# Ten feed-forward blocks by seven products, and the residual added inside PSUM

## The chip, the cores and the metric

The kernel runs on one core of a Trainium2 chip. The metric is the device time of one execution in microseconds. Five engines work side by side, each through its own queue in order: TensorE (PE in the profile; its weight loads are shown apart as PEld), VectorE (DVE), ScalarE (ACT), GpSimd (POOL), and SyncE (SP), which here only issues transfers. Matmuls write to PSUM, an accumulator memory of eight banks, each holding a 128x512 fp32 tile; VectorE and ScalarE read and write it as they do the main on-chip memory, SBUF.

## The reference

Two layers of a hybrid decoder trunk on 256 tokens with a model width of 2048, all in fp32. Cut to what matters here:

```python
for l in range(DEPTH):                       # 2
    h = rms_norm(x, norm1_g[l])
    z = h @ w_in[l]
    ...                                      # gating unit and windowed attention
    x = x + mixed @ w_out[l]
    h2 = rms_norm(x, norm2_g[l])
    x = x + (jax.nn.silu(h2 @ w_gate[l]) * (h2 @ w_up[l])) @ w_down[l]
```

The feed-forward width is 5632, that is, 11 blocks of 512 columns. The change is all in the last line: how `h2 @ w_gate` and `h2 @ w_up` are multiplied out, and how the product with `w_down` is added to x.

## The kernel before

**Precision.** A matmul takes its operands as rounded fp32 (`F32R`). To keep fp32 accuracy every operand is split into a rounded part and the remainder, and a product is three matmuls: high by high, high by low, low by high (`mm3`, lines 133 to 136). Weights are split on the chip: `split2` (line 89) has ScalarE write the rounded part `wh` (line 95) and VectorE the remainder `wl` (line 96), for a loaded piece `raw` of 128 x 1024. There are six `raw`, five `wh` and four `wl` buffers.

**The unit.** `unit` (line 138) loads one piece, splits it and multiplies it with two activation blocks for both halves of the tokens: 12 matmuls of 128x512. `product` (line 152) strings units to an accumulation over the whole depth.

**Stages of a layer.** The w_in products with attention and gating between them; the w_out products (`add_part`, line 527), each added to the residual `xres` by VectorE; then the feed-forward part. `norm_block` (line 478) sums the squares of a finished piece of x on ScalarE and transposes it for the next product.

**Seven products.** The gate and up products of one block, with tokens in two halves, make a 2 x 2 product of blocks. `seven` (line 564) computes it with seven block products in place of eight, after a scheme of Strassen's kind: five products need sums of weights (VectorE, lines 590, 591 and 596; a sixth operand is completed by an accumulating transfer that POOL issues, line 598) and sums of activations (`ext`, made once in `combine`). They go in half-units of 6 matmuls (`s_unit`): four steps of five half-units into five PSUM banks `m0` to `m4`, then eight half-units into two further tiles `n0` and `n1`. At the end ScalarE and VectorE combine the banks (lines 607 to 615, 628 to 631), apply Silu, and the two results `sg` are transposed and split again by `act_T` (line 550), into one of eight `aT` buffers.

**Standard work.** Blocks 0 and 1 are done with eight products by `gate_up` (line 651). `down` (line 666) multiplies finished blocks with w_down: for each of four column groups n it takes a pair of accumulators, runs two units per block, and VectorE adds the pair onto `xres` (line 685). While the seven-product stream runs, these accumulators come from the pool `pd`, which holds one pair (`dacc`); after it they come from `pa` (`acc`).

**What sets the order.** The seven-product stream loads VectorE more than TensorE; standard units load TensorE more. The two are interleaved by a running debt: `vec` adds the estimated VectorE time of an instruction to it (1.14 or 0.6 us), `pe` takes off the matmul time (0.227 us each times `LOAD`, 0.95). Whenever the debt is over zero after a half-unit, units of the standard stream are written in. The standard stream runs in a fixed sequence, `STD_ORDER` (line 43): gate-up of block 0, down of 0 and 2, gate-up of 1, then four more downs. A down whose blocks aren't ready gives nothing. `later` and `tick` write delayed work (the transposes) in after a count of units. On top of this order the framework's scheduler places each engine's instructions.

Of the kernel before, what the change touches and what calls it, by code (L numbers as in the profile page):

```python
# [12 lines left out]
F32 = mybir.dt.float32  # L13
# [3 lines left out]
ALU = mybir.AluOpType  # L17
# [33 lines left out]
UNIT_AT = (6, 9, 12, 15, 19, 23)  # L51

# [12 lines left out]
def trunk(ctx, tc, x, xt, w_in, w_out, w_gate, w_up, w_down, sgu_w, sgu_g, consts,  # L65
# [39 lines left out]
    def vec(n, cost=VEC):  # L105
        debt[0] += n * cost
# [7 lines left out]
    def later(delay, fn):  # L114
        pending.append((clock[0] + delay, next(serial), fn))
# [8 lines left out]
    def new_acc(pool=pa, tag="acc"):  # L124
        return [pool.tile([P, NB], F32, tag=tag, name=f"{tag}{t}") for t in range(NTOK)]
# [7 lines left out]
    def mm3(acc, ah, al, wh, wl, first, last):  # L133
        nc.tensor.matmul(acc, ah, wh, start=first, stop=False)  # L134
        nc.tensor.matmul(acc, ah, wl, start=False, stop=False)  # L135
        nc.tensor.matmul(acc, al, wh, start=False, stop=last)  # L136

    def unit(src, acts, acc, first, last):
        raw = raw_load(src, 2 if clock[0] < 4 else 1)
        wh, wl = split2(raw)  # L140
        for j in range(2):
            act, aj = acts[j]
            for t in range(NTOK):
                ts = slice(t * P, (t + 1) * P)
                mm3(
                    acc[t], act[:, 0, aj, ts], act[:, 1, aj, ts], wh[:, j, :], wl[:, j, :],
                    first and j == 0, last and j == 1,
                )
        pe(12)
        tick()  # L150
# [100 lines left out]
    for lay in range(L):  # L251
# [305 lines left out]
            pe(2)  # L557
            pairs_f.setdefault(b, []).append(pair)

        def act_later(b, sg, act_T=act_T):  # L560
            for c in range(2):
                later(2 + c, lambda c=c: act_T(b, c, sg))

        def seven(b, lay=lay, pairs2=pairs2, ext2=ext2, act_later=act_later):
            bank = [pa.tile([P, NB], F32, tag="acc", name=f"m{i}") for i in range(5)]

            def s_unit(raw, m, i, op, first, last):
                wh, wl = split2(raw)
                for j in range(2):
                    ah, al = (op(2 * i + j, h) for h in range(2))  # L570
                    mm3(bank[m], ah, al, wh[:, j, :], wl[:, j, :], first and j == 0, last and j == 1)
# [34 lines left out]
            m1 = zp.tile([P, NB], F32, tag="z", name="m1")  # L606
            nc.scalar.copy(m1, bank[0])
            u1 = zp.tile([P, NB], F32, tag="z", name="u1")
            nc.vector.tensor_tensor(u1, bank[3], m1, ALU.add)
            c22 = zp.tile([P, NB], F32, tag="z", name="c22")  # L610
            c21 = zp.tile([P, NB], F32, tag="z", name="c21")
            nc.vector.tensor_tensor(c21, bank[2], u1, ALU.add)
            nc.vector.tensor_tensor(c22, bank[1], c21, ALU.add)
            nc.vector.tensor_tensor(u1, bank[1], u1, ALU.add)
            nc.vector.tensor_tensor(u1, bank[4], u1, ALU.add)
            vec(5, VEC_P)
            yield
            bank = [pa.tile([P, NB], F32, tag="acc", name=f"n{i}") for i in range(2)]
            for i in range(4):
                b21 = raw_load(w_gate[lay, b, i, 1])  # L620
                first, last = i == 0, i == 3
                s_unit(b21, 0, i, a_op(1, 0), first, last)
                yield
                s_unit(kept[i], 1, i, a_op(1, 1), first, last)
                yield
            sg = [m1, c21]
            for t, m in ((0, m1), (1, c21)):
                nc.vector.tensor_tensor(m, bank[t], m, ALU.add)
                nc.scalar.activation(m, m, AF.Silu, scale=rstd2[t])
            for t, c in ((0, u1), (1, c22)):  # L630
                nc.vector.scalar_tensor_tensor(sg[t], c, nrstd2[t], sg[t], ALU.mult, ALU.mult)
            vec(4, VEC_P)
            act_later(b, sg)
            yield

# [27 lines left out]
            vec(NTOK, VEC_P)  # L663
            act_later(b, sg)

        def down(blocks, final, lay=lay, pairs_f=pairs_f, norm_block=norm_block, ss1=ss1, pairs1=pairs1):
            for n in range(ND):
                while any(len(pairs_f.get(b, [])) < 2 for b in blocks):
                    yield False
                acc = new_acc() if seven_done[0] else new_acc(pd, "dacc")  # L670
                for k, b in enumerate(blocks):
                    for c in range(2):
                        pair = pairs_f[b][c]
                        unit(
                            w_down[lay, b, n, c], [(pair, 0), (pair, 1)], acc,
                            k == 0 and c == 0, k == len(blocks) - 1 and c == 1,
                        )
                        yield True
                for t in range(NTOK):
                    parts = 2 if final and lay == L - 1 and n == ND - 1 else 1  # L680
                    w = NB // parts
                    for i in range(parts):
                        cs = slice(n * NB + i * w, n * NB + (i + 1) * w)
                        xs = xres[:, t, cs]
                        nc.vector.tensor_tensor(xs, acc[t][:, i * w : (i + 1) * w], xs, ALU.add)  # L685
                        if final and lay == L - 1:
                            nc.sync.dma_start(out[t * P : (t + 1) * P, cs], xs)
                    vec(1, VEC_P)
                if final and lay < L - 1:
                    norm_block(n, ss1, pairs1, lay + 1, C_G1)  # L690

        def std_stream(gate_up=gate_up, down=down):
# [105 lines left out]
```

## Time and profile before

| | us |
|---|---|
| median of 3 runs | 1981.08 |
| lowest and highest | 1977.15, 1983.19 |
| the profiled execution | 1970.47 |
| its span, first to last instruction | 1968.8 |

The profile is of one execution. Its page begins with each engine's busy time in the span, and the clock that TensorE was granted in 40 slices (9 is 90% or more). A group row gives line, engine, operation, output and inputs, count, then the total busy time and the mean duration in ns of one, then the idle time of the engine just before and what ended it. Window rows give, for a stretch, the busy time and count of each engine in the order PE, PEld, DVE, ACT, POOL, then the clock, the DMA engines' busy share and their GB/s. Timeline rows give start and length in us, and in brackets an idle time before with what ended it. Durations of neighbours on one engine can overlap, so what an instruction costs its queue is the distance between two starts.

### The profile page before, as it was taken

The numbers are of one execution on the slowest core, as the hardware profiler recorded it, in microseconds if no ns is written. First come the engines' busy times: TensorE is split into PE (matmuls) and PEld (weight loads), VectorE is DVE, ScalarE is ACT, GpSimd is POOL, SyncE is SP. The second block draws the span as 40 slices with busy tenths as digits, with TensorE's granted clock in tenths as the row PEclk, the third lists the DMA queues.
The fourth block names the chain that finished last, engine by engine and source line by source line (L and its number), as shares of the span: only waits on it lengthen the run. The fifth ranks groups of instructions, "written<-read, shape, count | busy, mean of one in ns | idle before, by whom it ended". The sixth has DMA issues, their size and how long they took to land.

```text
span 1968.8 us, 24956 instructions
## 1 busy us (share of the span) xinstructions
PE 1942.7 (99%) x8884; PEld 1586.9 (81%) x8884; DVE 1678.4 (85%) x1812; ACT 1175.8 (60%) x1489; POOL 115.5 (6%) x116
## 2 busy tenths in 40 slices
PE   9999999999999999999999999999999999999999
PEld 6788888778887878888887888878788878888887
DVE  6665689999999999999856666899999999999996
ACT  7565566555565565565656755665656555655563
POOL 0210000000000000000002000000000000000000
PEclk9999999999999999999999999999999999999999
DMA  9544557667767668668555355576686776686684
GB/s 354 188 144 153 189 171 243 206 204 245 231 220 244 221 212 258 220 223 259 202 202 195 127 170 178 178 253 193 214 258 213 225 254 206 210 279 203 221 270 141
DMA packets 117805, 422.20 MB, mean 214 GB/s; under 512 B 13104, under 2 KB 13744, under 8 KB 117680
## 3 DMA queue, kind: packets, MB, share of 16 engines
q1 hardware_dynamic: 105264, 375.52, 53.2%
q0 software_dynamic: 12416, 45.09, 12.3%
q8 instruction: 69, 1.13, 0.2%
q14 instruction: 56, 0.46, 0.1%
HBM read 418.47 MB, written 2.10 MB: 214 GB/s over the span
## 4 chain that ended last, share of the span: by engine, by line
PE 85%; DVE 6%; issue 3%; ACT 2%; DMA 2%; POOL 1%; SPq 0%; DVEq 0%; ACTq 0%; POOLq 0%
PE dacc L134 9%; PE dacc L135 9%; PE dacc L136 9%; PE acc L135 8%; PE acc L136 8%; PE acc L134 8%; PE m L135 7%; PE m L136 7%; PE m L134 7%; PE n L135 3%; PE n L136 3%; PE n L134 3%; DVE wl L96 3%; ACT wh L95 1%; DVE raw L596 1%
## 5 line engine op out<-in xcount | busy, mean ns | idle before, releaser
L95 ACT CAST wh<-raw 128x1024 fp32r<-128x1024 f32 (+1 forms) x778 | 799.9, 1049 | 627.4 <-DVE raw L590 227.3
L96 DVE TENSOR_TENSOR wl<-raw,wh 128x1024 fp32r<-128x1024 f32 (+1 forms) x778 | 927.0, 1217 | 154.5 <-PE acc L135 75.9
L134 PE MATMUL dacc<-wh,aT 128*128 128x512 f32 x608 | 237.0, 392 | 0.2
L135 PE MATMUL dacc<-wl,aT 128*128 128x512 f32 x608 | 237.0, 390 | 0.0
L136 PE MATMUL dacc<-wh,aT 128*128 128x512 f32 x608 | 236.7, 390 | 0.0
L135 PE MATMUL m<-wl,ext 128*128 128x512 f32 x576 | 227.5, 395 | 4.7 <-DVE wl L96 4.7
L134 PE MATMUL m<-wh,ext 128*128 128x512 f32 x576 | 226.8, 394 | 4.8 <-ACT wh L95 4.8
L136 PE MATMUL m<-wh,ext 128*128 128x512 f32 x576 | 224.5, 390 | 0.0
L96 DVE TENSOR_TENSOR wl<-t,wh 128x1024 fp32r<-128x1024 f32 x144 | 175.5, 1219 | 16.0 <-issue 7.0
L95 ACT CAST wh<-t 128x1024 fp32r<-128x1024 f32 x144 | 151.4, 1051 | 49.5 <-PE dacc L136 31.6
L134 PE MATMUL acc<-wh,hT 128*128 128x512 f32 x448 | 179.4, 403 | 0.8 <-ACT wh L95 0.6
L135 PE MATMUL acc<-wl,hT 128*128 128x512 f32 x448 | 176.4, 394 | 1.2 <-DVE wl L96 1.1
L136 PE MATMUL acc<-wh,hT 128*128 128x512 f32 x448 | 175.6, 392 | 0.0
L598 POOL DMA_DIRECT2D t<-in_w_gate_dram x72 | 61.6, 855 | 1373.3 <-DVE wl L96 719.4
L134 PE MATMUL acc<-wh,aT 128*128 128x512 f32 x352 | 139.1, 395 | 0.0
L136 PE MATMUL acc<-wh,aT 128*128 128x512 f32 x352 | 137.3, 390 | 0.0
L135 PE MATMUL acc<-wl,aT 128*128 128x512 f32 x352 | 137.3, 390 | 0.0
L134 PEld LDWEIGHTS dacc<-wh,aT 128*128 128x128 f32 x608 | 114.1, 188 | 25.6 <-DVE xres L685 2.3
L135 PEld LDWEIGHTS m<-wl,ext 128*128 128x128 f32 x576 | 108.1, 188 | 32.0 <-DVE wl L96 10.7
L135 PEld LDWEIGHTS dacc<-wl,aT 128*128 128x128 f32 x608 | 114.2, 188 | 24.1 <-DVE wl L96 0.8
L136 PEld LDWEIGHTS dacc<-wh,aT 128*128 128x128 f32 x608 | 114.2, 188 | 23.7
L134 PEld LDWEIGHTS m<-wh,ext 128*128 128x128 f32 x576 | 108.2, 188 | 29.8 <-ACT wh L95 7.7
(145 smaller groups left out, 2974.3 us busy)
## 6 DMA issues: line engine op xcount, KB each, us to landing
raw<-in_w_gate_dram SPq DMA_DIRECT2D x176, 512.0 KB, 5.4
raw<-in_w_up_dram SPq DMA_DIRECT2D x176, 512.0 KB, 4.2
raw<-in_w_down_dram SPq DMA_DIRECT2D x176, 512.0 KB, 4.9
raw<-in_w_in_dram SPq DMA_DIRECT2D x108, 512.0 KB, 4.1
t<-in_w_gate_dram POOLq DMA_DIRECT2D x72, 512.0 KB, 5.9
raw<-in_w_out_dram SPq DMA_DIRECT2D x64, 512.0 KB, 3.3
bias<-in_band_dram POOLq DMA_DIRECT2D x8, 512.0 KB, 4.9
xr<-in_xt_dram SPq DMA_DIRECT2D x8, 256.0 KB, 6.1
```

The source lines that it names most:

```text
L95: nc.scalar.copy(wh[:, j : j + step, :], src)
L96: nc.vector.tensor_tensor(wl[:, j : j + step, :], src, f(wh[:, j : j + step, :]), ALU.subtract)
L134: nc.tensor.matmul(acc, ah, wh, start=first, stop=False)
L135: nc.tensor.matmul(acc, ah, wl, start=False, stop=False)
L136: nc.tensor.matmul(acc, al, wh, start=False, stop=last)
L596: nc.vector.tensor_tensor(b12, b12, b22, ALU.add)
L598: nc.gpsimd.dma_start(t2, w_gate[lay, b, i, 1], accum_op=ALU.add)
```

## The change

- Block 1 is computed by seven products too: ten blocks, and block 0 alone by `gate_up`.
- The fixed sequence is gone. `std_stream` looks which blocks have both their transposed pairs: with two or more ready (or with the last of them) it runs a down over two, at most three, blocks; else gate-up of block 0 if it is still to do; else it gives nothing.
- `down` has ScalarE copy the pieces of x into the accumulator pair, the matmuls add onto them (none of them starts a new sum), and ScalarE copies the pair back to `xres`. VectorE has no part in it.
- The last products of `seven` are added onto banks 0 and 2 in place of two new tiles, after these have been read; one VectorE addition falls away, and the last two half-units of each step change places.
- A transpose is held back while all eight `aT` tiles are in use, and released as a down gives tiles free.
- `LOAD` 0.95 becomes 0.97; seven `raw` buffers in place of six; the scratch memory for POOL's transfer descriptors is halved.

```diff
-S_BLOCKS = (2, 3, 4, 5, 6, 7, 8, 9, 10)
-STD_ORDER = (
-    ("gu", 0), ("down", (0, 2)), ("gu", 1), ("down", (1, 3, 4)), ("down", (5, 6, 7)), ("down", (8, 9)), ("down", (10,)),
-)
+S_BLOCKS = (1, 2, 3, 4, 5, 6, 7, 8, 9, 10)
+GU_BLOCKS = tuple(b for b in range(NFF) if b not in S_BLOCKS)
+CHUNK = (2, 3)
+ACT_TILES = 8
...
-LOAD = 0.95
+LOAD = 0.97
...
-        raw = wp.tile([P, 2, NB], F32, tag="raw", name="raw", bufs=6)
+        raw = wp.tile([P, 2, NB], F32, tag="raw", name="raw", bufs=7)
...
+        held = []
+        live = [0]
+
+        def release(live=live, held=held, act_T=act_T):
+            while held and live[0] < ACT_TILES:
+                live[0] += 1
+                act_T(*held.pop(0))
...
             for c in range(2):
-                later(2 + c, lambda c=c: act_T(b, c, sg))
+                def ready(c=c):
+                    held.append((b, c, sg))
+                    release()
+
+                later(2 + c, ready)
...
+                s_unit(b22, 4, i, e_op(3), first, last)
+                yield
                 s_unit(b12, 2, i, e_op(0), first, last)
                 yield
-                s_unit(b22, 4, i, e_op(3), first, last)
-                yield
                 kept.append(t2)
...
-            nc.scalar.copy(m1, bank[0])
...
-            nc.vector.tensor_tensor(u1, bank[3], m1, ALU.add)
...
-            nc.vector.tensor_tensor(c21, bank[2], u1, ALU.add)
+            nc.scalar.copy(m0, bank[0])
+            nc.vector.tensor_tensor(m0, bank[3], m0, ALU.add)
+            nc.vector.tensor_tensor(c12, bank[1], m0, ALU.add)
+            nc.vector.tensor_tensor(c12, bank[4], c12, ALU.add)
+            nc.vector.tensor_tensor(c21, bank[2], m0, ALU.add)
             nc.vector.tensor_tensor(c22, bank[1], c21, ALU.add)
...
-            bank = [pa.tile([P, NB], F32, tag="acc", name=f"n{i}") for i in range(2)]
             for i in range(4):
                 b21 = raw_load(w_gate[lay, b, i, 1])
-                first, last = i == 0, i == 3
-                s_unit(b21, 0, i, a_op(1, 0), first, last)
+                s_unit(b21, 0, i, a_op(1, 0), False, i == 3)
                 yield
-                s_unit(kept[i], 1, i, a_op(1, 1), first, last)
+                s_unit(kept[i], 2, i, a_op(1, 1), False, i == 3)
                 yield
-            sg = [m1, c21]
-            for t, m in ((0, m1), (1, c21)):
-                nc.vector.tensor_tensor(m, bank[t], m, ALU.add)
-                nc.scalar.activation(m, m, AF.Silu, scale=rstd2[t])
-            for t, c in ((0, u1), (1, c22)):
+            nc.vector.tensor_tensor(m0, bank[2], m0, ALU.add)
+            sg = [zp.tile([P, NB], F32, tag="z", name="sg0"), m0]
+            for t, c in ((0, bank[0]), (1, m0)):
+                nc.scalar.activation(sg[t], c, AF.Silu, scale=rstd2[t])
+            for t, c in ((0, c12), (1, c22)):
                 nc.vector.scalar_tensor_tensor(sg[t], c, nrstd2[t], sg[t], ALU.mult, ALU.mult)
...
             for n in range(ND):
-                while any(len(pairs_f.get(b, [])) < 2 for b in blocks):
-                    yield False
                 acc = new_acc() if seven_done[0] else new_acc(pd, "dacc")
+                for t in range(NTOK):
+                    nc.scalar.copy(acc[t], xres[:, t, n * NB : (n + 1) * NB])
...
+                        if n == ND - 1:
+                            live[0] -= 1
+                            release()
...
-                        nc.vector.tensor_tensor(xs, acc[t][:, i * w : (i + 1) * w], xs, ALU.add)
+                        nc.scalar.copy(xs, acc[t][:, i * w : (i + 1) * w])
...
-            for k, (kind, what) in enumerate(STD_ORDER):
-                if kind == "gu":
-                    yield from gate_up(what)
+            gus = list(GU_BLOCKS)
+            downed = set()
+            while left[0]:
+                full = [b for b in sorted(pairs_f) if len(pairs_f[b]) == 2 and b not in downed]
+                rest = left[0] == len(full)
+                if len(full) >= CHUNK[0] or rest:
+                    blocks = full[: CHUNK[1]]
+                    downed.update(blocks)
+                    yield from down(blocks)
+                elif gus:
+                    yield from gate_up(gus.pop(0))
                 else:
-                    yield from down(what, k == len(STD_ORDER) - 1)
+                    yield False
...
-    nc = bacc.Bacc("TRN2", target_bir_lowering=False, num_devices=1, dynamic_dma_scratch_size=8192)
+    nc = bacc.Bacc("TRN2", target_bir_lowering=False, num_devices=1, dynamic_dma_scratch_size=4096)
```

More of the change, by code (lines that the diff above doesn't have):

```diff
@@ L131, in small_ps, with mm3, unit @@
         return pool.tile(shape, F32, tag=tag, name=name)
[L133 to L138, printed above, removed]
+    def mm3(acc, ah, al, wh, wl, first, last, again=False):
+        nc.tensor.matmul(acc, ah, wh, start=first, stop=False, skip_group_check=again)
+        nc.tensor.matmul(acc, ah, wl, start=False, stop=False, skip_group_check=again)
+        nc.tensor.matmul(acc, al, wh, start=False, stop=last, skip_group_check=again)
+    def unit(src, acts, acc, first, last, again=False):
         raw = raw_load(src, 2 if clock[0] < 4 else 1)
@@ L146, in unit @@
                     acc[t], act[:, 0, aj, ts], act[:, 1, aj, ts], wh[:, j, :], wl[:, j, :],
-                    first and j == 0, last and j == 1,
+                    first and j == 0, last and j == 1, again,
                 )
@@ L570, in s_unit @@
                     ah, al = (op(2 * i + j, h) for h in range(2))
-                    mm3(bank[m], ah, al, wh[:, j, :], wl[:, j, :], first and j == 0, last and j == 1)
+                    mm3(
+                        bank[m], ah, al, wh[:, j, :], wl[:, j, :], first and j == 0,
+                        last and j == 1, m in (0, 2),
+                    )
                 pe(6)
```

32 lines of the change are left out of this document (16 added, 16 removed).

## The prediction

> **What bounds the kernel now.** I read the head of the page first, then windows over the feed-forward part, then the groups by form, then the timeline where TensorE stalls.
>
> ```profile
> span 1968.8 us, 24956 instructions
> PE 1942.7 (99%) x8884; PEld 1586.9 (81%) x8884; DVE 1678.4 (85%) x1812; ACT 1175.8 (60%) x1489; POOL 115.5 (6%) x116
> PEclk9999999999999999999999999999999999999999
> PE 85%; DVE 6%; issue 3%; ACT 2%; DMA 2%; POOL 1%; SPq 0%; DVEq 0%; ACTq 0%; POOLq 0%
> ```
>
> TensorE is busy nearly all the time at full clock and carries 85% of the chain of waits. VectorE's 85% is a mean over unlike stages, so the next rows are two feed-forward parts and three blocks of seven products.
>
> ```profile
> 290.00:960.00 670.00, 663.19 (x2941) 541.78 (x2940) 635.88 (x622) 402.35 (x429) 31.54 (x37) 1.00 0.72 230
> 1270.00:1964.00 694.00, 687.85 (x3051) 562.52 (x3050) 648.57 (x637) 408.16 (x434) 31.53 (x37) 1.00 0.71 225
> 555.00:628.00 73.00, 70.75 (x316) 57.35 (x315) 69.27 (x67) 43.46 (x48) 3.41 (x4) 1.00 0.68 221
> 702.00:776.00 74.00, 73.17 (x327) 59.80 (x326) 71.45 (x72) 44.13 (x48) 3.44 (x4) 1.00 0.71 228
> 849.00:922.00 73.00, 73.00 (x326) 60.21 (x326) 70.03 (x68) 43.77 (x47) 3.41 (x4) 1.00 0.74 236
> ```
>
> The columns are the stretch, its length, busy time and instructions of PE, weight load, DVE, ACT and POOL, the clock, and the DMA share. In a block DVE is busy 70 of 73 us, so it comes a hair behind PE; ACT is idle 40% of the time. PE is idle 6.8 us in the first part and 6.2 us in the second. Those 13 us are what any better pacing can win, and what a worse one adds to.
>
> The pitch (start to start) of a 128x512 matmul and of VectorE's two sizes:
>
> ```profile
> 257.17 0.39 PE L136 MATMUL acc<-wh,aT 128*128 128x512 f32 x1
> ...
> 262.84 0.39 PE L134 MATMUL acc<-wh,aT 128*128 128x512 f32 x1
> ```
>
> Twenty-five matmuls lie between these starts: 5.67 / 25 = 0.227 us each. The durations of 0.39 overlap and are not the price.
>
> ```profile
> 596.43 1.22 DVE L96 TENSOR_TENSOR wl<-raw,wh 128x1024 fp32r<-128x1024 f32 x1
> 597.56 0.68 DVE L555 TENSOR_TENSOR aT<-ps_f,aT 128x512 fp32r<-128x512 f32 x1
> 598.16 1.21 DVE L596 TENSOR_TENSOR raw<-raw 128x1024 f32<-128x1024 f32 x1
> 599.30 1.22 DVE L96 TENSOR_TENSOR wl<-t,wh 128x1024 fp32r<-128x1024 f32 x1
> ```
>
> So DVE takes 1.13 us for 128x1024 and 0.60 for 128x512, each about 0.08 under its duration.
>
> **The change part by part.**
>
> *Block 1 by seven products.* A block done the standard way is 16 units of 12 matmuls, 192; by seven products it is 28 half-units of 6, 168. One block in each layer changes over, so 48 matmuls go: 48 x 0.227 = -10.9 us on the engine that sets the end. In the instruction order PE has 4200 rows from one layer's first product to the next one's, against 4224. The transposes stay as many.
>
> The same block costs DVE more. These are the rows that price it and what is taken away:
>
> ```profile
> L96 DVE TENSOR_TENSOR wl<-raw,wh 128x1024 fp32r<-128x1024 f32 x774 | 924.3, 1219 | 152.7 <-PE acc L135 75.9 <-issue 34.6 <-ACT wh L95 21.0
> L590 DVE TENSOR_TENSOR raw<-raw 128x1024 f32<-128x1024 f32 x72 | 88.1, 1224 | 2.3
> L685 DVE TENSOR_TENSOR xres<-dacc,xres 128x512 f32<-128x512 f32 x60 | 39.3, 682 | 0.5 <-PE dacc L136 0.2
> L685 DVE TENSOR_TENSOR xres<-acc,xres 128x512 f32<-128x512 f32 x18 | 12.3, 687 | 10.3 <-PE acc L136 10.3
> L628 DVE TENSOR_TENSOR m<-n,m 128x512 f32<-128x512 f32 x18 | 12.3, 682 | 0.0
> L631 DVE SCALAR_TENSOR_TENSOR m<-u,nr,m 128x512 f32<-128x512 f32 x18 | 13.4, 743 | 0.0
> L660 DVE SCALAR_TENSOR_TENSOR sg<-dacc,ir,sg 128x512 f32<-128x512 f32 x8 | 5.6, 741 | 0.0
> ```
>
> Added to DVE in a layer: 12 splits (28 for 16) and 12 weight sums, 24 x 1.135 = 27.2 us, and the new block's ending, 6 x 0.60 + 2 x 0.66 = 4.9. Taken away: the residual additions, (78 x 0.60 + 4 x 0.34) / 2 = 24.1; one of two L628 additions in nine blocks, 5.4; two L660, 1.3. Net 32.1 - 30.8 = +1.3 us: DVE works as long as before while PE has 5.4 us less. So the question is whether DVE still hides.
>
> *Work by readiness, load 0.97.* The filler work (units of the standard gate and of the down projection) now amounts to 104 units a layer in place of 120, over ten blocks in place of nine. The instruction order gives a typical block 9 units, 276 matmuls and 8 transposes; before it was 12, 312 and 8. In PE time 276 x 0.227 + 8 x 0.11 = 63.5 us (before 71.7; a transpose is 0.11, below). In DVE time 28 + 9 splits x 1.135, 12 sums x 1.14, 6 x 0.60, 2 x 0.66 and 2 x 0.60: 61.8 us (before 68.2). The spare falls from 3.5 to 1.7 us a block: PE stays the bound, closely. Where filler runs short, DVE falls behind. Before, such a stretch shows itself here:
>
> ```profile
> 595.62 0.27 PE L199 MATMUL ps_f<-ident,sg 128*128 128x128 f32 x1
> 596.44 0.49 PE L134 MATMUL m<-wh,ext 128*128 128x512 f32 x1 [0.54 <-ACT wh L95]
> 597.70 0.50 PE L135 MATMUL m<-wl,ext 128*128 128x512 f32 x1 [0.77 <-DVE wl L96]
> 600.56 0.50 PE L134 MATMUL m<-wh,ext 128*128 128x512 f32 x1 [0.77 <-ACT wh L95]
> 708.79 0.27 PE L199 MATMUL ps_f<-ident,m 128*128 128x128 f32 x1
> 708.90 0.27 PE L199 MATMUL ps_f<-ident,c 128*128 128x128 f32 x1
> ```
>
> By counts from the order times the pitches, that stretch without filler holds 3.3 us more DVE work than PE work, and PE lost 0.54 + 0.77 + 0.77 = 2.1 us; the other 1.2 us was covered by the splits that the four wl buffers hold ready. The order has, per layer, three such stretches where there were four: -4.5 us at the start (before -5.3), -4.0 after the eighth block, 84 matmuls on end, and -6.4 around the ninth, 126 matmuls (before -3.3, -4.2 and -4.2 further on); all others are at -3.0 or better. With the same cover 3.3 + 2.8 + 5.2 = 11.3 stand against 4.1 + 2.1 + 3.0 + 3.0 = 12.2 (the trace has 6.5 of idle per layer, so the cover is mostly larger, for both alike). I put 0 for the difference, between -6 (half of the 13 us of idle time gone) and +10 (the 5.2 of the longest stretch in each layer, with nothing won elsewhere). The two last half-units of each step change places, which moves no issue and no DMA past another.
>
> *Residual through PSUM on ScalarE.* Before each of the 24 groups of a layer two 128x512 copies of x go into the accumulators, and after it two come back. No copy into PSUM is in the trace; the nearest rows are PSUM to SBUF and SBUF to SBUF.
>
> ```profile
> L554 ACT CAST aT<-ps_f 128x512 fp32r<-128x512 f32 x44 | 25.7, 583 | 20.1 <-PE ps_f L199 11.6 <-PE dacc L136 8.6
> L607 ACT COPY m<-m 128x512 f32<-128x512 f32 x18 | 10.4, 579 | 0.5 <-PE m L136 0.4
> L206 ACT ACTIVATE void<-xres 128x512 bf16<-128x512 f32 x32 | 19.9, 622 | 0.7 <-DMA xres<-in_x_dram 0.3
> 849.23 0.58 ACT L607 COPY m<-m 128x512 f32<-128x512 f32 x1
> 874.87 0.72 ACT L629 ACTIVATE m<-m,ir 128x512 f32<-128x512 f32 x1
> 875.49 0.70 ACT L629 ACTIVATE c<-c,ir 128x512 f32<-128x512 f32 x1
> ```
>
> A copy is 0.58 to 0.62 long, and as L629 shows the next starts 0.10 sooner: 0.48 to 0.52 of the queue. Some 97 of them and 12 casts at 0.95 are 58 us a layer on an engine busy 405 of 690: 68%, hidden as work. As a wait it is another matter. The copy out waits for a group's last matmul, and behind it in ACT's queue stand the copies in and the casts, for which DVE's splits and then PE wait. From the wait's end the worst case is four copies, 1.9 us, a cast, 0.95, a split, 1.14, and 0.2 of matmul tail: 4.2 us. The order has the next cast's matmul at least 22 rows, 5.0 us, after that last matmul, 34 rows in the median: covered. If that cover is gone, 4.2 us at one group. The accumulators themselves are one pair: out 0.58 and in 0.58 plus tail is 1.4 us, and the order leaves 6 to 134 matmuls between the groups, 3 once, besides the 3 by which the first of the pair is done sooner (0.7 us). So 6 rows give 2.0 us: enough; only the one with 3 lacks a little. I take +1 us for both layers, between 0 and 24 (below). The old evictions made PE wait little; then a row of the DMA issues and one of the timeline at the end, for what follows:
>
> ```profile
> PEld dacc L134 <- DVE xres L685: 2.3, 6, 0.4
> t<-in_w_gate_dram POOLq DMA_DIRECT2D x72, 512.0 KB, 5.9
> 1963.71 1.43 DVE L685 TENSOR_TENSOR xres<-acc,xres 128x256 f32<-128x256 f32 x4 [4.07 <-PE acc L136]
> ```
>
> *The rest.* The accumulating transfers on POOL become 80, one more quarter is read for each, 8 x 0.52 MB in all; each is read eight half-units (11 us) or more after its issue and lands in 5.9, and the DMA share is 0.72: nothing, or 5.9 us each if that cover went. A smaller descriptor scratch can at worst set these transfers one behind another; they are issued a step of five half-units apart. A seventh raw buffer lets SP run further ahead: 0, or a little off the idle time. Keeping two of five banks for all products takes two additions and a wait away, and adds one: the next block's first product waits for the Silu out of bank 0, 0.72 long, under six matmuls, 1.4 us. Held transposes come at once in the order, so nothing. The four last copies take about what L685 takes at the end: 0.
>
> **Sum.** -10.9 + 0 + 1 = -9.9 us: span 1958.9, and with the 1.7 us around it (1970.47 - 1968.8) 1960.6. The median of the runs, 1981.08, stands 10.6 above the profiled execution; I carry that over: 1971.
>
> **The rivals.**
>
> *ScalarE's round trip shows at every group.* The 40 groups in the bodies share one pair of accumulators, and the copies sit in a queue in order. If the 6 matmuls don't count as cover because casts hold ACT up, each costs 1.4 less 0.7, 0.6 us: +24, 1995. At 0.25 us each it is +10 and the gain is gone: 1981. For it: ACT's casts already follow PE closely (L554 lost 8.6 us waiting behind dacc). Against it: 22 rows of casts done ahead. The Trainium skill, Perfetto Trace Analysis, section Optimizing Tensor Performance, says that independent groups should rotate through PSUM banks, so that emptying one overlaps the next group's matmuls. That rule speaks against this pair, which gains a second trip; by it the time would be the 1995, while the row of 2.3 us above shows the one-way trip nearly hidden.
>
> *DVE becomes the bound.* It has 1.7 us spare per block. In the block at 555 PE lost 2.25 us with 3.2 spare. If handovers cost DVE 2.7 us a block, 20 blocks get 1 us longer: +20 - 10.9, 1990. It decides from 2.2 us a block on (0.5 x 20 eats the gain). For it: 70.03 of 73 busy; against it: at 849 PE loses nothing at all.
>
> *Pacing better than before.* Half of the 13 us idle goes besides: 1964.
>
> **How the numbers follow.** Forecast 61%, by itself 1966 to 1976. Round trip in part 14% (1981), in full 8% (1995); DVE bound 10% (1990); better pacing 7% (1964). A difference of 0.3%, 5.9 us, is about what a measurement of this kernel tells from none, so faster means under 1975.1 and slower over 1987. Faster 0.61 less its upper edge plus 0.07, 0.64; slower 0.08 + 0.10 less a little, 0.17; same the rest, 0.19. The range takes in better pacing and the partial round trip and stops at the edge of the slow ones: 1963 to 1987.
>
> **What would show it.** Right: some 48 fewer big matmuls, PE idle in the feed-forward parts near 13 us, DVE near 97% in a block, ACT near 68%. Wrong: PE waiting for ACT's copies into dacc summed to over 10 us, or L134 and L135 waiting for wh or wl at more places than the two long stretches of a layer.

## The result, and the profile after

| | before | after |
|---|---|---|
| median of 4 runs each, us | 1979.99 | 1966.79 |
| lowest and highest | 1977.15, 1983.19 | 1964.53, 1967.48 |
| ratio, with its 95% interval | | 0.9931 (0.9913 to 0.9949) |
| the profiled execution | 1970.47 | 1966.23 |
| its span | 1968.8 | 1964.5 |

The fourth run of before came with the result; its profiled execution is not among the four. The changed kernel is faster by 13.2 us in the medians, but by 4.3 us only between the two profiled executions. The head of the page after:

```profile
span 1964.5 us, 24978 instructions
...
PE 1935.3 (99%) x8836; PEld 1576.1 (80%) x8836; DVE 1676.7 (85%) x1772; ACT 1289.0 (66%) x1709; POOL 123.3 (6%) x124
...
PE 80%; DVE 10%; issue 4%; ACT 3%; DMA 2%; POOL 1%; DVEq 0%; SPq 0%; ACTq 0%; POOLq 0%
```

The 48 matmuls are gone (8884 to 8836). VectorE's busy time stayed, as its added and removed work cancel, but its share of the chain of waits rose from 6% to 10%: more of the chain runs through it. The two feed-forward parts, as windows (columns as before):

```profile
290.00:960.00 670.00, 662.16 (x2929) 538.71 (x2928) 642.27 (x614) 453.72 (x526) 34.97 (x41) 1.00 0.76 234
1270.00:1960.00 690.00, 682.12 (x3015) 554.64 (x3013) 645.44 (x616) 462.62 (x541) 34.95 (x41) 1.00 0.74 227
```

TensorE is idle 7.8 and 7.9 us there, against 6.8 and 6.2 before. VectorE is busy 642.27 / 670 = 95.9% of the first, ScalarE 67.7%. The costliest groups that answer to the terms of the sum:

```profile
L96 DVE TENSOR_TENSOR wl<-raw,wh 128x1024 fp32r<-128x1024 f32 x782 | 933.5, 1220 | 142.4 <-PE acc L135 81.2 <-issue 23.1 <-ACT wh L95 15.6
...
L686 ACT COPY dacc<-xres 128x512 f32<-128x512 f32 x80 | 46.6, 592 | 1.0
L705 ACT COPY xres<-dacc 128x512 f32<-128x512 f32 x80 | 46.4, 583 | 31.5 <-PE dacc L136 30.9
```

The copy into PSUM, which no trace showed before, is 0.592 us long. ScalarE waits 30.9 us in front of the copies out. To see whether anyone waits for ScalarE in turn, I read TensorE's waits (total, times, longest), those of before first:

```profile
PE m L134 <- ACT wh L95: 4.8, 8, 0.8
PE m L135 <- DVE wl L96: 4.7, 7, 0.8
```

and those of after, the last row being the weight load's:

```profile
PE m L135 <- DVE wl L96: 6.6, 10, 1.6
...
PE m L134 <- ACT wh L95: 3.2, 4, 1.0
PE ps_f L199 <- DVE m L643: 2.4, 2, 1.2
...
PE dacc L134 <- ACT aT L554: 1.6, 2, 0.8
...
PEld dacc L134 <- ACT dacc L686: 2.8, 10, 0.4
```

The copies into the accumulators hold weight loads for 2.8 us in all; among the matmuls' own waits they have no row. The row of 1.6 us is one wait in each layer: a down begins before the cast of its own transposed block has ended. What holds TensorE most is VectorE's remainder `wl`, in few and longer waits. Where the longest lie, the timeline of TensorE in the first layer shows (rows with an idle time in front):

```profile
748.96 0.50 PE L135 MATMUL m<-wl,ext 128*128 128x512 f32 x1 [0.66 <-DVE wl L96]
751.91 0.50 PE L134 MATMUL m<-wh,ext 128*128 128x512 f32 x1 [0.96 <-ACT wh L95]
...
766.78 0.50 PE L135 MATMUL m<-wl,ext 128*128 128x512 f32 x1 [0.52 <-DVE wl L96]
...
864.81 0.50 PE L135 MATMUL m<-wl,hT 128*128 128x512 f32 x1 [1.65 <-DVE wl L96]
...
877.08 0.33 PE L199 MATMUL ps_f<-ident,m 128*128 128x128 f32 x1 [1.20 <-DVE m L643]
...
878.21 0.49 PE L135 MATMUL m<-wl,ext 128*128 128x512 f32 x1 [0.17 <-DVE wl L96]
...
880.48 0.50 PE L134 MATMUL m<-wh,ext 128*128 128x512 f32 x1 [0.61 <-ACT wh L95]
```

All but the third lie in the two long stretches without filler that the prediction named, after the eighth block (84 matmuls, 735 to 757) and around the ninth (126, 851 to 886). The wait at 766.78 comes just behind the first, when filler has run again: VectorE had been idle for 3.3 us before 761.37, behind a cast of ScalarE that waited 4.6 us for a w_down transfer. VectorE stands back to back while TensorE waits for it at 864.8:

```profile
862.95 0.68 DVE L629 TENSOR_TENSOR c<-m,c 128x512 f32<-128x512 f32 x1
863.55 1.21 DVE L96 TENSOR_TENSOR wl<-t,wh 128x1024 fp32r<-128x1024 f32 x1
864.68 1.22 DVE L96 TENSOR_TENSOR wl<-raw,wh 128x1024 fp32r<-128x1024 f32 x1
```

ScalarE's casts wait for such transfers in before and in after (before first):

```profile
ACT wh L95 <- DMA raw<-in_w_down_dram: 19.9, 20, 2.7
ACT wh L95 <- DMA raw<-in_w_down_dram: 17.6, 7, 4.7
```

Before has 5.7 us more for w_up and w_gate, after 0.2. In the kernels of experiments 3 and 6 these waits are gone but for 0.6 and 0 us.

**The whole account.** Waiting lists leave out what overlapping durations hide, so I took the distances from start to start of all TensorE records in the two stretches between a layer's first and last seven-product matmul. For a 128x512 matmul, what the distance to the next start has beyond 0.227 us is a small gap (up to 0.12) or a large one, and the few thousandths by which some distances fall short are taken off the small ones. Transposes are counted from their start to the next start, so a wait of a matmul behind a transpose is in their row. The sums are good to about 0.1 us. They are shown also for two kernels that come below: experiment 6 (nine blocks) and experiment 3 (a down opens with one ready block).

| us, both layers together | before | after | experiment 6 | experiment 3 |
|---|---|---|---|---|
| transposes (176) | 23.4 | 22.2 | 16.4 | 16.4 |
| large gaps | 12.5 | 16.7 | 4.6 | 6.9 |
| small gaps | 10.4 | 13.8 | 10.4 | 13.6 |
| sum | 46.3 | 52.7 | 31.4 | 36.9 |
| 128x512 matmuls in the kernel | 8016 | 7968 | 8016 | 7968 |
| span | 1968.8 | 1964.5 | 1952.8 | 1947.2 |

From before to after the work gives -48 x 0.227 = -10.9 and the sum +6.4: together -4.5, and the spans differ by -4.3. So more than half of the saved work was lost again in waits inside the seven-product stream. The other two columns close less well: from after to experiments 6 and 3 the sums give -10.4 and -15.8, the spans -11.7 and -17.3, so 1.3 and 1.5 us lie outside the stretches.

### The profile page after: what moved, and what is told of

Same layout as the page of the kernel before. It is cut to its first block, busy times and chain, and to the rows that moved or that the text cites. A ratio compares the mean times of both kernels' runs of the same rounds, so it can differ in the third digit from the quotient of the medians.

```text
span 1964.5 us, 24978 instructions
## 1 busy us (share of the span) xinstructions
PE 1935.3 (99%) x8836; PEld 1576.1 (80%) x8836; DVE 1676.7 (85%) x1772; ACT 1289.0 (66%) x1709; POOL 123.3 (6%) x124
## 4 chain that ended last, share of the span: by engine, by line
PE 80%; DVE 10%; issue 4%; ACT 3%; DMA 2%; POOL 1%; DVEq 0%; SPq 0%; ACTq 0%; POOLq 0%
PE m L135 10%; PE m L136 10%; PE m L134 10%; PE dacc L134 8%; PE dacc L135 8%; PE dacc L136 8%; PE acc L135 8%; PE acc L136 8%; PE acc L134 7%; DVE wl L96 5%; ACT wh L95 2%; DVE raw L605 1%; DMA raw<-in_w_down_dram 1%; POOL ir L182 1%; DVE raw L611 1%
## 5 line engine op out<-in xcount | busy, mean ns | idle before, releaser
L134 PE MATMUL m<-wh,ext 128*128 128x512 f32 x640 | 251.6, 394 | 3.4 <-ACT wh L95 3.2
L135 PE MATMUL m<-wl,ext 128*128 128x512 f32 x640 | 251.2, 393 | 2.6 <-DVE wl L96 2.6
L134 PE MATMUL dacc<-wh,aT 128*128 128x512 f32 x640 | 250.6, 397 | 2.8 <-ACT aT L554 1.6
L135 PE MATMUL dacc<-wl,aT 128*128 128x512 f32 x640 | 251.0, 392 | 0.0
L136 PE MATMUL dacc<-wh,aT 128*128 128x512 f32 x640 | 250.0, 391 | 0.0
L136 PE MATMUL m<-wh,ext 128*128 128x512 f32 x640 | 249.8, 390 | 0.0
L96 DVE TENSOR_TENSOR wl<-t,wh 128x1024 fp32r<-128x1024 f32 x160 | 195.1, 1219 | 13.7 <-issue 7.8
L135 PE MATMUL m<-wl,hT 128*128 128x512 f32 x480 | 187.8, 391 | 4.0 <-DVE wl L96 4.0
L95 ACT CAST wh<-t 128x1024 fp32r<-128x1024 f32 x160 | 168.1, 1050 | 33.5 <-PE dacc L136 18.8
L136 PE MATMUL m<-wh,hT 128*128 128x512 f32 x480 | 187.0, 390 | 0.0
L134 PE MATMUL m<-wh,hT 128*128 128x512 f32 x480 | 186.6, 391 | 0.1
L134 PEld LDWEIGHTS m<-wh,ext 128*128 128x128 f32 x640 | 120.2, 188 | 31.1 <-ACT wh L95 6.7
L135 PEld LDWEIGHTS m<-wl,ext 128*128 128x128 f32 x640 | 120.2, 188 | 30.1 <-DVE wl L96 5.6
```

Of the source, the lines that this page charges most:

```text
L95: nc.scalar.copy(wh[:, j : j + step, :], src)
L96: nc.vector.tensor_tensor(wl[:, j : j + step, :], src, f(wh[:, j : j + step, :]), ALU.subtract)
L134: nc.tensor.matmul(acc, ah, wh, start=first, stop=False, skip_group_check=again)
L135: nc.tensor.matmul(acc, ah, wl, start=False, stop=False, skip_group_check=again)
L136: nc.tensor.matmul(acc, al, wh, start=False, stop=last, skip_group_check=again)
```

## The experiments

Experiments 1 to 4 ran as one set on one chip, 5 to 8 as a second set on that chip, 9 to 12 on another. Each set has its own runs of the kernel before, with medians of 1971.98 (13 runs), 1973.87 (14) and 1971.49 (7). My theory before the first of them: the changes beside the tenth block are a good gain, and the tenth block runs the filler dry and spends much of it. The rival: ScalarE's round trip through PSUM is what costs, at every group.

### 1. The kernel before, again

No edit. The question was whether the 10 us between its runs and its profiled execution are its own.

> The kernel before, unchanged, profiled once more. Two readings of the result are open: the profiled spans differ by 4.3 us (1968.8 to 1964.5), the medians by 13.2 (1979.99 to 1966.79). If the profiled 1970.47 was a low draw of the kernel before, this profile has a span near 1977 with the extra us spread, or a granted clock under 1.000. If the profiled one is typical, the span is 1969 again and the medians differ for a reason that the trace doesn't hold. Ratio 1.000.

Measured: 1972.39 (10 runs), ratio 1.0002 (0.9993 to 1.0012), profiled span 1969.9. Here the profiled execution, 1971.65, lies amid the runs. So the +10.6 that the prediction carried from the profiled time to the median belonged to the runs of that first set, not to the kernel.

### 2. The pace of before in the kernel after

```diff
-LOAD = 0.97
+LOAD = 0.95
```

> The changed kernel with LOAD back at 0.95: the debt asks for more filler per half-unit, and by the instruction order the filler runs out twice in each layer, for 186 and for 252 matmuls on end, with 11.5 and 16.8 us more VectorE than TensorE work (4.0 and 6.4 with 0.97). Filler theory: these are lost but for 1 to 2 us of cover each, some 18 us a layer beyond now, about 2003 us. Rival (the waits come from ScalarE's copies at the ends of groups, not from filler): the same 24 groups a layer, so 1967 within 4 us.

Measured: 2043.07, ratio 1.0361 (1.0345 to 1.0376). TensorE's waits:

```profile
PE m L134 <- ACT wh L95: 19.0, 33, 1.4
PE m L135 <- DVE wl L96: 18.3, 28, 1.6
PE ps_f L199 <- DVE m L643: 14.9, 10, 3.1
PE dacc L134 <- ACT dacc L686: 5.8, 7, 1.2
```

The end of the first layer's stream, as a row of TensorE's timeline and as a window:

```profile
994.24 0.48 PE L199 MATMUL ps_f<-ident,m 128*128 128x128 f32 x1 [3.14 <-DVE m L643]
...
993.50:1000.50 7.00, 5.58 (x17) 4.31 (x18) 2.07 (x4) 1.17 (x2) 0.00 (x0) 0.54 0.47 155
```

The smaller constant asks for more filler per half-unit; the ready blocks are eaten early, and the instruction order then has stretches of 186 and 252 matmuls without filler in each layer, in which VectorE has 11.5 and 16.8 us more to do than TensorE (after: 84 and 126, 4.0 and 6.4). By distances these two lose 10.3 and 15.2 us in the first layer, within 2 us of their excess, as expected. The direction was right and the whole loss twice as large, because I had counted these two alone. Two further stretches, of 102 and 120 matmuls, lose 4 us each, and the filler's own matmuls some 5 us more than after. Where the stream ends no filler is left: the last transposes wait (3.14 us above), and behind them the granted clock falls to 0.5 for some 7 us (0.54 in the window). By the account, about 16 us more than after lie outside the streams, in both layers together. Two hundredths of a pacing constant are worth 77 us here, so "work by readiness" and "0.97" can't be priced apart.

### 3. Downs open with one ready block

```diff
-CHUNK = (2, 3)
+CHUNK = (1, 3)
```

> The changed kernel with a down allowed from one ready block on (CHUNK (1, 3)): by the order no stretch is worse than -2.4 us after the first of a layer. Filler theory: the 2.4 us lost at 749 to 767 and the 4.3 us at 865 to 880, and the same in layer 2, go for the most part: 8 to 12 us less, about 1957. Rival (ScalarE's copies): more groups of fewer blocks mean more round trips, so 1967 or up to 5 us more.

Measured: 1948.65 (1948.34 to 1950.18), ratio 0.9885 (0.9868 to 0.9901). It is the fastest kernel of this study, 23 us under before and some 17 under the kernel after, more than the 8 to 12 expected. Head and chain of waits:

```profile
PE 1931.3 (99%) x8836; PEld 1575.3 (81%) x8836; DVE 1677.3 (86%) x1772; ACT 1337.0 (69%) x1805; POOL 122.3 (6%) x124
...
PE 90%; issue 3%; DVE 2%; ACT 2%; POOL 1%; DMA 1%; SPq 0%; ACTq 0%; DVEq 0%; POOLq 0%
```

the first feed-forward part as a window:

```profile
290.00:960.00 670.00, 668.65 (x2964) 544.79 (x2963) 645.37 (x616) 483.84 (x586) 35.05 (x41) 1.00 0.75 236
```

and TensorE's waits:

```profile
PE dacc L134 <- ACT wh L95: 1.4, 6, 0.3
...
PE m L135 <- DVE wl L96: 0.7, 2, 0.4
PE dacc L134 <- ACT dacc L686: 0.3, 2, 0.2
...
PEld dacc L134 <- ACT dacc L686: 5.5, 18, 0.6
```

The matmuls and VectorE's work are the same as after (x8836, x1772). Only the order differs: a lone ready block may be taken, no stretch has over 60 matmuls without filler, and the wait for `wl` falls from 6.6 to 0.7 us. ScalarE has 96 instructions more, 48 of the copies in and 48 out, since shorter downs make more groups. If the round trip cost at every group, this kernel would be the slower one; it is the faster. Its weight loads wait 5.5 us for the copies, against 2.8 after, but the matmuls themselves wait only 0.3 us. That rival falls here. The Trainium skill, Perfetto Trace Analysis, section Optimizing Tensor Performance, would have independent groups rotate through PSUM banks; this trace reuses a single pair with a read and a write between groups at 0.3 us of the matmuls' own waits, while matmuls of the other stream, in other banks, run in between.

### 4. Ten blocks, with the residual added by VectorE again

```diff
-                for t in range(NTOK):
-                    nc.scalar.copy(acc[t], xres[:, t, n * NB : (n + 1) * NB])
...
-                            False, k == len(blocks) - 1 and c == 1, True,
+                            k == 0 and c == 0, k == len(blocks) - 1 and c == 1,
...
-                        nc.scalar.copy(xs, acc[t][:, i * w : (i + 1) * w])
+                        nc.vector.tensor_tensor(xs, acc[t][:, i * w : (i + 1) * w], xs, ALU.add)
...
+                    vec(1, VEC_P)
```

> The changed kernel with the old eviction: no copy of x into PSUM, VectorE adds the accumulators onto x. VectorE gets back 24 us a layer, and by the order the filler runs out four times a layer, at -7.4, -16.8, -21.8 and -5.4 us. Filler theory: 35 us or so more lost per layer, about 2030 us: ten blocks don't pay without the relief of VectorE. Rival (ScalarE's round trip is what costs now): faster than the changed kernel, 1955 to 1965.

Measured: 2080.1, ratio 1.055 (1.0534 to 1.0565). TensorE's waits:

```profile
PE m L134 <- ACT wh L95: 30.5, 53, 1.4
PE m L135 <- DVE wl L96: 27.3, 32, 1.7
PE dacc L134 <- DVE xres L703: 15.8, 12, 3.5
PE ps_f L199 <- DVE m L643: 14.7, 12, 2.0
```

About 56 us of VectorE's time return (1732.4 busy against 1676.7) and the kernel loses 115 us: the additions also raise the debt, which asks for filler that isn't there, and stretches of 252 and 330 matmuls follow. Without ScalarE's part ten blocks can't be paced like this. The amount, over twice what I expected, holds this loss of order too, so it is no price of the VectorE work alone.

### 5. The kernel after, again

No edit.

> The changed kernel, unchanged, beside the kernel before on the chip of this set. From the traces: 48 matmuls less (-10.9 us), in the feed-forward parts some 3.4 us more lost in gaps over 0.12 us and 3.5 us more in small ones between matmuls: 4 to 6 us faster than the kernel before, so 1964 to 1968 if that is at 1972. If the 13 us of the first medians are the change's own, 1959.

Measured: 1965.53 (1963.99 to 1966.23), ratio 0.9957 (0.9943 to 0.9972): 8.3 us under before in the same set. The profiled span is 1963.8, 6.1 under that of before in experiment 1. So the gain is 4 to 8 us in all comparisons but the first set's medians, where before alone stood higher.

### 6. The kernel after with nine blocks

```diff
-S_BLOCKS = (1, 2, 3, 4, 5, 6, 7, 8, 9, 10)
+S_BLOCKS = (2, 3, 4, 5, 6, 7, 8, 9, 10)
```

> The changed kernel with S_BLOCKS from 2 on: nine blocks by seven products, blocks 0 and 1 the standard way, all else as changed. 48 matmuls more (+10.9 us) and 32 units more of filler; the order's worst stretch after the first is -2.9 us. Filler theory: the 10 us that the changed kernel loses to its two long stretches in both layers go, so the two sides cancel: 1965 within 3 us. Rival (the tenth block pays in full, waits have another cause): the changed kernel's time + 10.9, 1976.

Measured: 1955.08 (1953.83 to 1956.01), ratio 0.9905 (0.9891 to 0.992). The head of its page:

```profile
PE 1937.6 (99%) x8884; PEld 1586.8 (81%) x8884; DVE 1617.1 (83%) x1712; ACT 1237.7 (63%) x1619; POOL 115.7 (6%) x116
```

the first feed-forward part:

```profile
290.00:960.00 670.00, 669.25 (x2981) 548.28 (x2980) 615.47 (x589) 438.43 (x504) 31.62 (x37) 1.00 0.73 232
```

and TensorE's waits for the splits, which stood at 6.6 and 1.2 after:

```profile
PE m L135 <- DVE wl L96: 0.7, 2, 0.4
PE dacc L134 <- ACT wh L95: 0.2, 1, 0.2
```

Both forecasts missed, 1965 and 1976, and the kernel is faster than either. This settles the main question. With 48 matmuls more than after, the kernel is 10.5 us faster. So the tenth block, placed as it is, does not save its 10.9 us but costs 10.5, a loss of 21.4 in waits; the account above has 52.7 - 31.4 = 21.3 for it (20.5 with the profile of experiment 5). And everything else in the change gains 18.8 us over before (1973.87 - 1955.08), where the forecast had a cost of 1. VectorE is relieved: 615 of 670 us instead of 642. This price of the tenth block holds for downs over two ready blocks or more: nine blocks with downs from one ready block on were not run, so what the tenth block is worth in the order of experiment 3 is not shown.

### 7. ScalarE's copies alone, in the kernel before

```diff
+                for t in range(NTOK):
+                    nc.scalar.copy(acc[t], xres[:, t, n * NB : (n + 1) * NB])
...
-                            k == 0 and c == 0, k == len(blocks) - 1 and c == 1,
+                            False, k == len(blocks) - 1 and c == 1, True,
...
-                        nc.vector.tensor_tensor(xs, acc[t][:, i * w : (i + 1) * w], xs, ALU.add)
+                        nc.scalar.copy(xs, acc[t][:, i * w : (i + 1) * w])
...
-                    vec(1, VEC_P)
```

> The kernel before, with its nine blocks, fixed sequence and LOAD 0.95, and only the residual moved: x copied into PSUM by ScalarE, matmuls added onto it, ScalarE copying back. Theory that VectorE's relief is worth time only as room for a tenth block: the PE work is the same, the order's stretches without filler are like before (-3.3, -3.3, -3.6), so 1969 to 1972. Rival (ScalarE's round trip shows at every group): 20 groups a layer at up to 0.6 us, up to 24 us slower, 1980 to 1996.

Measured: 1976.56 (10 runs), ratio 1.0018 (1.0008 to 1.0029): a loss of 2.7 us, between my theory's gain and the rival's cost. TensorE's waits:

```profile
PE m L135 <- DVE wl L96: 6.0, 9, 0.8
PE m L134 <- ACT wh L95: 3.5, 6, 0.8
...
PE n L135 <- DVE wl L96: 2.4, 4, 0.7
```

VectorE is busy 46 us less (1632.3 against 1678.4), yet TensorE still waits for `wl`. The copies themselves hold its matmuls for 0.5 us. The edit also takes the additions out of the debt and so moves the filler. Relief alone wins nothing in the fixed sequence: VectorE is late in places, not on the whole.

### 8. One ready block, and less filler asked for

```diff
-CHUNK = (2, 3)
+CHUNK = (1, 3)
...
-LOAD = 0.97
+LOAD = 0.99
```

> A down from one ready block on and LOAD 0.99, so filler is asked for a little less often. By the order the worst stretch is -3.0 us, as against -2.4 with 0.97. Filler theory: 1949 within 3 us, since PE has few gaps left to win. Rival (VectorE is now the bound, so less filler per block starves PE): 1955 or more.

Measured: 1963.36 (1961.37 to 1964.03), ratio 0.9946 (0.9933 to 0.9959). My theory missed, and the time lies in the rival's range: no stretch is over 60 matmuls, and still 15 us went. TensorE's waits name another place:

```profile
PE dacc L134 <- ACT wh L95: 7.7, 22, 0.4
```

The timelines of ScalarE, VectorE and TensorE show how one such wait comes about:

```profile
442.24 2.01 ACT L95 CAST wh<-raw 128x1024 fp32r<-128x1024 f32 x2 [1.28 <-DVE raw L611]
448.06 1.99 ACT L95 CAST wh<-raw 128x1024 fp32r<-128x1024 f32 x2 [3.81 <-DVE raw L605]
...
443.20 3.49 DVE L96 TENSOR_TENSOR wl<-raw,wh 128x1024 fp32r<-128x1024 f32 x3
446.73 1.23 DVE L605 TENSOR_TENSOR raw<-raw 128x1024 f32<-128x1024 f32 x1
...
450.11 0.73 PE L134 MATMUL dacc<-wh,aT 128*128 128x512 f32 x2 [0.44 <-ACT wh L95]
```

The matmuls that wait 22 times are now the filler's own. A weight sum (L605) stands behind three splits until 446.73; ScalarE's next cast needs that sum and waits 3.81 us for it; behind it in ScalarE's queue stands the cast of a filler unit, whose matmul at 450.11 comes late. Here the filler itself is held up behind the engine to which it should give time.

### 9. Nine blocks at the pace of before

Experiment 6 with `LOAD` 0.95.

> Nine blocks by seven products with all else as changed (1955 us), and LOAD back at 0.95. With nine blocks there is filler enough for 0.95 too: by the order no stretch after the first is worse than -3.1 us. Theory P (the 19 us that nine blocks with the other edits gain over the kernel before come from the pacing by 0.97): 1970 or more. Theory Q (they come from VectorE's relief, downs by readiness and the reused banks, and 0.97 matters only where filler is scarce): 1953 to 1960.

Measured: 1957.97, ratio 0.9929 (0.9914 to 0.9944), as expected. Against 0.9905 of experiment 6 the constant is worth some 3 us (5 by the ratios, whose intervals overlap). With nine blocks there is filler enough for either pace; with ten the same step costs 77.

### 10. Nine blocks, the last products in tiles of their own

```diff
+            own = [pa.tile([P, NB], F32, tag="acc", name=f"n{i}") for i in range(2)]
...
-                s_unit(b21, 0, i, a_op(1, 0), False, i == 3)
+                s_unit(b21, 0, i, a_op(1, 0), i == 0, i == 3, own)
...
-                s_unit(kept[i], 2, i, a_op(1, 1), False, i == 3)
+                s_unit(kept[i], 1, i, a_op(1, 1), i == 0, i == 3, own)
...
+                nc.vector.tensor_tensor(m, own[t], m, ALU.add)
```

with a second ScalarE copy of bank 0 in each block (before has one), and with the added VectorE instruction counted in the debt.

> Nine blocks, all else as changed, but the last products of a block go into two further tiles again, with one VectorE addition more in each block and a second ScalarE copy out of bank 0. If the reused banks carry a good part of the 19 us: 18 blocks at 0.6 us of VectorE and its waits, 1962 to 1968. If not: 1955 to 1958.

Measured: 1959.08 (1957.83 to 1960.7), ratio 0.9935 (0.9921 to 0.995). That is between the two forecasts. Adding onto the kept banks is worth 4 to 6 us (times, ratios) against experiment 6. The two ratios' intervals only just part, and of the 6.0 us between the spans only 3.4 lie in the seven-product stretches, so its size is no firm figure.

### 11. The kernel before at the new pace

```diff
-LOAD = 0.95
+LOAD = 0.97
```

> The kernel before with LOAD 0.97 alone. Theory P (pacing): 1955 to 1962. Theory Q (VectorE, still with the residual, has no spare for less filler; the order's stretches are -5.4, -4.2 and -2.8): 1972 to 1985, no gain.

Measured: 1987.17, ratio 1.0074 (1.0055 to 1.0094). TensorE's longest waits for splits:

```profile
PE dacc L134 <- ACT wh L95: 6.8, 8, 2.2
PE n L135 <- DVE wl L96: 6.1, 6, 1.4
```

The longest of them, 2.2 us at 320.86, stands behind this cast:

```profile
319.76 1.04 ACT L95 CAST wh<-raw 128x1024 fp32r<-128x1024 f32 x1 [2.23 <-DMA raw<-in_w_gate_dram]
```

In before the step from 0.95 to 0.97 costs 15.7 us: of the two paces 0.95 is its better one. No stretch here is over 60 matmuls either, so a list of the longest stretches would not have shown this loss; one part of it is a late transfer into one of six `raw` buffers. The gain of experiment 6 is therefore not the constant by itself.

### 12. One ready block, a little more filler

Experiment 3 with `LOAD` 0.965.

> Ten blocks, a down from one ready block on, LOAD 0.965. 0.99 was 15 us worse than 0.97: ScalarE's casts came late behind VectorE's weight sums. If 0.97 lies between two slopes and is still on the side of too little filler, 0.965 gains: 1942 to 1947. If it is at the bottom: 1949 to 1954, since the order has five stretches of -2 to -3 us in place of two.

Measured: 1955.54 (1954.81 to 1956.49), ratio 0.9917 (0.9902 to 0.9932), above both forecasts and slower than 0.97 by 6 to 7 us (ratios 0.9917 and 0.9885). Of 0.965, 0.97 and 0.99, the value 0.97 is the best with downs from one ready block on. Experiment 3 stays the fastest.

## Why the prediction came out as it did

The time was near, 1971 forecast and 1966.79 measured, and that was in part luck: two terms were wrong and partly cancelled. What was right is the work saved and the price of ScalarE's copies.

- **Block 1, -10.9 us.** Right as work: 48 matmuls fewer, and VectorE's total unchanged (1676.7 against 1678.4).
- **Work by readiness and pace, put at 0 between -6 and +10.** This term failed: all that is not the work of block 1 measured +6.4 in the seven-product streams, inside the range but far from 0. The two long stretches were sized about right: 2.8 + 5.2 predicted, and by start-to-start distances 2.4 and 4.3 us are lost in the first layer at 749 to 767 and 864 to 881 (0.7 of the 2.4 at 766.78, behind a late transfer). The error was in the comparison. I subtracted a modelled 12.2 us for before, whose trace showed 6.5 a layer, and took the cover to be larger "for both alike". It isn't: of the 3.3 us modelled for the stretch of 25 matmuls at a layer's start the trace after shows 0.2 (at 306), of the long ones' 8.0 it shows 6.7. Nor does the length decide alone: in before the stretches of 42 and 41 matmuls at 393 and 590, with a block's transposes in them, lose 2.9 and 3.2 us, and the stretch of 60 at 569 loses nothing. The modelled 8.0 of the long ones against the measured 6.5 would have given +1.5 a layer; small gaps, 13.8 against 10.4, are the rest, and their cause stays open.
- **The same term hides two larger ones.** By experiment 6 the edits beside the tenth block gain 18.8 us and the tenth block gives 10.5 of it back. The forecast saw neither; VectorE's net +1.3 us a layer showed an even balance, and that balance was of totals. If the parts simply add up, the 18.8 are 3 to 5 for the pace (experiment 9) and 4 to 6 for the kept banks (experiment 10), though experiment 11 shows that the pace alone costs time in before. The remaining 8 to 12 would be shared by downs taken as blocks are ready, held transposes, the relief of VectorE and the seventh buffer. ScalarE's copies alone lose 2.7 (experiment 7), so if they pay, it is together with others. How these share it was not tried, nor were six buffers and the scratch size. The seventh buffer is a rival that stays open: ScalarE's casts wait 25.6 us for feed-forward weights in before (18.7 in experiment 1), while experiment 6 has no row of it. Most of that is idle time of ScalarE, but in before two waits of TensorE in the first layer (0.6 us at 377 and 0.5 at 554, by distances) stand behind such late transfers.
- **ScalarE's copies, +1 (0 to 24).** Right: 0.592 and 0.583 us long against 0.58 to 0.62 bounded; 2.8 us of weight loads held for them, and 2.7 us lost where they came alone (experiment 7).
- **Bank reuse, at 0.** A gain of 4 to 6 in experiment 10 by the medians, 3.4 of it in the streams.
- **The carry of +10.6 to the median.** Wrong. After's profiled 1966.23 lies amid its runs, and experiment 1 shows that before's does too in another set. In the profiled time the forecast of 1960.6 was 5.6 too low, and the carry 10 too high: so 1971 came out near the median by luck. Why before's first runs stood at 1977 to 1983 stays open.
- **The rivals.** ScalarE's round trip falls by experiment 3. "DVE becomes the bound" holds in places: TensorE waits for `wl` mostly where filler is missing, 6.6 us in all, and 0.7 us in experiment 3. Its price per block was a mean, where the loss sits in two places a layer. "Pacing better than before" is what experiment 3 became, by changing one number.
- **What was to show it.** VectorE 95.9% of the first feed-forward part (near 97 forecast in a block), ScalarE 67.7% (68), waits for copies under 10 us, and the long waits of the seven-product matmuls in or just behind the two long stretches: all came. A few small waits for splits lie elsewhere, the largest 0.4 us at 342, so the sign of being wrong showed faintly. TensorE's idle time, 15.7 us for "near 13", was the sign that the pacing term was too low.

## What to carry to other kernels

Where two streams are interleaved so that one hides the other's engine, first ask whether the filler is there whenever it is asked for: list the stretches without it in the written order and compare them with the measured loss of the stretches that the kernel already has, not with a model of them. The list is not enough by itself: in experiments 8 and 11 time went with no long stretch in the order. A saving that uses up filler can cost more than it saves, as the tenth block did, and the cheapest cure may be the condition that opens the filler (here one ready block in place of two, 17 us). A pacing constant is tuned to one order: the same step from 0.95 to 0.97 was worth -77, -3 and +16 us in three kernels.

## What the runs showed that was not expected

- The page's busy time of TensorE hides gaps. It fell by 7.4 us (1942.7 to 1935.3) where 10.9 us of work went, since durations of 0.39 at a pitch of 0.227 swallow gaps up to 0.16 us. Only distances from start to start gave an account that closes, to 0.2 us from before to after and to 1.5 for the other two kernels.
- Transposes are cheap when nothing holds them: 16.4 / 176 = 0.093 us each in experiments 3 and 6. The 0.133 in before (23.4 / 176) is not theirs: there the matmuls right behind four transposes of the first layer wait for splits, 0.6 to 1.0 us from start to start. In the kernel after a transpose waits itself, at 877.08, for VectorE's last product of a block.
- A copy into PSUM was as long as a copy out of it, 0.592 against 0.583 us, and the account above, in which matmuls onto copied x count 0.227 us like all others, closes: no price of adding onto such data shows in it.
